# Attention scores over 64 queries of two heads and 192 keys, and a head in another order with the first group's third stage set by set

## The chip, the cores and the metric

The kernel runs on one core of one Trainium2 chip. The metric is the device time of one execution in microseconds. The profile is one further execution, taken by the hardware profiler. Of the core's engines, TensorE (PE) does the matrix products; its weight loads are listed apart as PEld. VectorE is DVE, ScalarE is ACT and GpSimd is POOL. SP only issues DMA transfers; the queues on which an engine issues them are written SPq, ACTq and so on.

## The reference

One decoder layer over 2048 tokens of width 1024, in fp32. What it computes, cut to what matters here:

```python
mod = silu(c) @ w_ada + b_ada;  shift, scale, gate = split(mod)
u = x * (1 + scale) + shift                              # (2048, 1024)
q, k, v, a_gate, p_in, p_gate, m_a, m_p = split(u @ w_in)
# 16 query heads on 2 key heads, head width 64; each query sees its last 128 keys
logits = q @ k.T / 8 + bias[query - key]; masked outside of the window
probs = softmax([logits, sink])[:-1]
a = (probs @ v * silu(a_gate)) @ w_attn_proj
p = ((pool(p_in) @ w_pool_mix) * pool_scale * silu(p_gate)) @ w_pool_proj
y = ((sigmoid(m_a) * a + sigmoid(m_p) * p) @ w_out) * (1 + gate)
out = layer_norm(alpha * x + y)
```

`silu(c) @ w_ada` is one vector times a matrix: 1024 shifts, 1024 scales and 1024 gates. The input u, and with it everything else, needs the shifts and scales first.

## The kernel before

**Products.** Every large product is done on 2 by 2 blocks with seven products in place of eight. A `Quad` holds two column tiles of 128 outputs and computes them over two halves of 512 tokens. Its moving operands are the seven `sets` B11, T1, T2, B21, T3, B22 and T4: differences and sums of the blocks of u, each held as a high and a low part (`hi`, `lo`), so that three products of reduced precision make one of full precision (`mm3`). One of the seven products is 12 instructions of 128x512. `plan` lists all products in one row of numbers; a product is the tick to which everything else is tied. The stages of a quad are F (B11, T1), S (T2, B21), Th (T3, B22) and L (T4). Quads go in groups of two or alone; in a group of two, a stage is done for the first quad and then for the second. `split_part` makes hi (ACT) and lo (DVE or POOL) of the weights some products ahead, `behind` evacuates what a product has made, and `at`, `defer` and `steps` tie other work to a product's number. Within an engine all instructions keep the order in which the program writes them.

**Phases.** The tokens go in two chunks of 1024. In each chunk there is a first phase (k, v, the first queries, two gates), an attention phase named o0 or o1 (13 quads alone, with attention laid over their products) and a phase for the rest of the projections with the pooling. After both chunks come the output projections and the layer norm.

**Attention.** `overlay` does 64 steps a chunk, one for each block of 128 queries and pair of heads. A `beat` after every quarter of a product decides when the next step comes. In `step(n)`, PE makes the scores of step n (`scores`), the transposes of step n-2 (`transposes`) and the values of step n-3 (`values`). In the program's names, `qs` are the queries, `kk` the keys (hi and lo stacked over each other on 128 partitions), `lg` the bank for scores, `bt` the bias, `L` the probabilities, `pt` the bank for transposes, `pth` and `ptl` their high and low parts, `vv` the values and `pv` the bank for the result. A step's scores are four products: two heads by hi and lo of the keys, each of 128 queries by 256 keys. ACT takes exp and scales, DVE adds the bias and finds the minimum, and makes `ptl`.

**The head.** `head` runs before the first quads and its order is written out by hand. `load(k)` fetches for each of the eight tiles of 128 channels the columns of w_ada for shift and scale and the tokens. `pe_modulation(k)` makes the tile's shifts on PE, in eight products with one moving column; in the trace they are 16 records. `modulation(k)` makes its scales on DVE, as a sum over products with `cb`, which is c spread over all partitions, and then adds the shift. Then come the modulated x, the differences, and the parts of the sets. `idle_products(n)` are n products with no use, put where PE would otherwise be idle. The products of the first two stages of the first group are written out piece by piece (`products`, `more`). After the head, `fold_parts` multiplies a pooling matrix into its weights in 16 folds, each on `pt` or `pv`, and `gate_modulation` makes the gates.

Of the kernel before, what the change touches and what calls it, by code (L numbers as in the profile page):

```python
# [19 lines left out]
P = 128  # L20
# [7 lines left out]
HD = 64  # L28
# [31 lines left out]
def kernel(  # L60
# [30 lines left out]
    BF16 = mybir.dt.bfloat16  # L91
    set_names = ("B11", "T1", "T2", "B21", "T3", "B22", "T4")
# [7 lines left out]
    nsink = cp.tile([P, HEADS], F32, name="nsink")  # L100
# [7 lines left out]
    e_rep = dp.tile([P, HEADS, ET], F32, name="e_rep")  # L108
# [24 lines left out]
    q_d = dp.tile([2, KT, 2, 2, P, CH], F32, name="q_d")  # L133
# [34 lines left out]
    class Pools:  # L168
        def __init__(self, name, **bufs):
            self.name, self.bufs, self.turns = name, {"c": 4, "p": 2, **bufs}, {}  # L170
            self.fresh = True
# [140 lines left out]
    now, due, hooks = [0], [], {}  # L312
# [139 lines left out]
    def behind(ph, q, kind, h):  # L452
        if kind == "F":
            if h == 0:
                q.c = bank(("lg", "c1")[q.x] if q.pair else "mm")
                if q.x and ph.fresh:
                    t = sets["B11"][:, 0, 0, :]
                    mm(q.c, t[:, 0:P], t, start=True, stop=True, skip_group_check=True)
                    ph.fresh = False
# [16 lines left out]
        else:  # L476
            q.consume(ph, 1, 0, q.c)

    def run(phases, products, before, loads):
        starts = {z["first"]: z for z in phases}  # L480
        ph, leave, beat = None, None, None
        for p, (q, kind, h, name) in enumerate(products):
# [29 lines left out]
            if done:  # L512
                if kind == "S":
                    behind(ph, q, kind, h)
# [3 lines left out]
            else:  # L518
# [4 lines left out]
                behind(ph, q, kind, h)  # L523
# [24 lines left out]
    def kv_quad(s):  # L548
        def keep_k(ph, t, src):
# [3 lines left out]
            defer(2, lambda: [sp.dma_start(cols(k_d[s, :, n, :], t), as32(x)) for n, x in enumerate((hi, lo))])  # L553

        def turn_v(ph, t, vt):
# [8 lines left out]
            defer(2, lambda: [sp.dma_start(v_d[s, :, a, NB * t : NB * (t + 1)], v[:, a]) for a in range(2)])  # L564

        def consume(ph, mi, t, src):
            if mi == 0:
                keep_k(ph, t, src)
            else:
                vt = ph.own("vt") if s == 0 else cols(ph.spare(), 0)  # L570
                act.activation(vt, src, AF.Copy, scale=0.5)
                defer(2, lambda: turn_v(ph, t, vt))

        return Quad((win[TK], win[TV]), consume)

    def q_quad(s, m):
        def consume(ph, mi, t, src):
            hi, lo = ph.c("q_hi", F32R), ph.c("q_lo", F32R)
            act.activation(hi, src, AF.Copy, scale=-0.125)
            dve.scalar_tensor_tensor(lo, src, -0.125, as32(hi), ALU.mult, ALU.subtract)  # L580
            defer(2 if m else 1, lambda: [sp.dma_start(q_d[s, m + mi, t, n], as32(x)) for n, x in enumerate((hi, lo))])
# [184 lines left out]
    def spread_bias(j, q):  # L766
        q.dma_start(e_rep[:, 2 * j : 2 * j + 2, :], e_d[2 * j : 2 * j + 2, :].partition_broadcast(P))

    def overlay(ph, s, n_slots):
# [4 lines left out]
        kvt, qts, bts = {}, {}, {}  # L774
        marks, Es, Ls, pts, xs, pvs, outs, ags, kept = {}, {}, {}, {}, {}, {}, {}, {}, {}
# [20 lines left out]
        def load_q(h):  # L796
# [821 lines left out]
```

## Time and profile before

| | us |
|---|---|
| median of 3 runs (lowest to highest) | 1700.26 (1699.17 to 1703.98) |
| the profiled execution | 1703.35 |
| its span in the profile | 1701.2 |
| PE busy | 1665.3 |
| first real product on PE | 22.29 |
| first and last score of the first chunk | 161.69, 471.5 |
| first and last score of the second chunk | 743.3, 1049.9 |

The profiled execution lies within the range of the three runs. In a row of the timeline there stand the start, the length from the first start to the last end, the engine, the tiles and the number of instructions. A row of grouped instructions has their busy time, the mean length of one in ns, and the idle time before them with what ended it. Almost everything goes through a helper on line 56, so tiles tell the rows apart, not lines.

### The profile page before, as it was taken

What the parts mean: (1) busy time and instruction counts of PE and PEld (TensorE: products, weight loads), DVE (VectorE), ACT (ScalarE), POOL (GpSimd) and SP (SyncE); (2) the same over time, 40 slices, a digit from 0 to 9 for tenths busy, and PEclk for the clock granted to TensorE, in tenths of its full rate; (3) what the DMA queues carried; (4) which work ended last, traced back from release to release, by engine and by line L of the source; (5) the groups of instructions that cost most, each with busy time, mean ns of one, the idle gap of its engine ahead of it and who ended that gap; (6) DMA issues with size and microseconds to landing.
All of it is one profiled execution on the core that took longest, in us unless ns stands there. A gap on an engine that the chain in (4) does not pass through costs nothing.

```text
span 1701.2 us, 24948 instructions
## 1 busy us (share of the span) xinstructions
PE 1665.3 (98%) x8112; PEld 1397.0 (82%) x8112; DVE 1185.1 (70%) x2167; ACT 988.4 (58%) x1943; POOL 589.4 (35%) x563
## 2 busy tenths in 40 slices
PE   9899999999999999999999999999999999999997
PEld 7788888888788888888888888888888888888886
DVE  6855666666647778656666666487876785778878
ACT  4645888787853336358877787333544453434553
POOL 3013454545462223323424333322242211113544
PEclk9899999999999999999999999999999999999999
DMA  9489676776557889865456454589968685777343
GB/s 358 151 294 311 202 225 217 242 239 208 170 178 223 264 288 326 289 206 157 150 171 215 156 175 135 190 280 326 329 238 309 197 312 201 261 264 281 149 149 124
DMA packets 236833, 389.50 MB, mean 229 GB/s; under 512 B 20872, under 2 KB 90528, under 8 KB 236576
## 3 DMA queue, kind: packets, MB, share of 16 engines
q1 hardware_dynamic: 231280, 382.36, 66.8%
q10 hardware_dynamic: 5392, 5.53, 1.0%
q8 instruction: 64, 1.05, 0.3%
q14 instruction: 65, 0.53, 0.1%
q0 software_dynamic: 32, 0.02, 0.0%
HBM read 243.63 MB, written 147.35 MB: 230 GB/s over the span
## 4 chain that ended last, share of the span: by engine, by line
PE 68%; ACT 11%; DVE 6%; issue 5%; DMA 3%; POOL 1%; SPq 1%; DVEq 0%; ACTq 0%; POOLq 0%
PE mm L56 43%; PE lg L56 11%; PE c L56 9%; ACT L L56 5%; PE pv L56 3%; PE pt L56 3%; DVE w_set L56 2%; ACT pth L56 2%; ACT w_set L56 1%; DVE wide L56 1%; ACT sig L56 1%; DVE p L56 1%; DVE ptl L56 1%; SPq L56 1%; ACT q_hi L56 0%
## 5 line engine op out<-in xcount | busy, mean ns | idle before, releaser
L56 PE MATMUL mm<-set_B,w_set 128*128 128x512 f32 x2664 | 652.7, 391 | 0.6 <-DVE w_set L56 0.6
L56 PEld LDWEIGHTS mm<-set_B,w_set 128*128 128x128 f32 x2664 | 496.6, 188 | 103.7 <-DVE w_set L56 1.5
L56 PE MATMUL mm<-set_T,w_set 128*128 128x512 f32 x1896 | 466.1, 392 | 1.5 <-POOL w_set L56 1.2
L56 POOL TENSOR_TENSOR W<-W 128x512 f32<-128x512 f32 x185 | 266.9, 1453 | 573.1 <-DVE w_set L56 394.0
L56 PEld LDWEIGHTS mm<-set_T,w_set 128*128 128x128 f32 x1896 | 351.5, 189 | 74.4 <-POOL w_set L56 2.5
L56 DVE TENSOR_TENSOR w_set<-W,w_set 128x1024 fp32r<-128x1024 f32 x197 | 254.5, 1292 | 110.5 <-ACT w_set L56 109.2
L56 ACT ACTIVATE L<-L 128x257 f32<-128x257 f32 (+3 forms) x512 | 241.4, 498 | 96.8 <-DVE L L56 96.3
L56 ACT CAST w_set<-W 128x1024 fp32r<-128x1024 f32 x222 | 232.2, 1047 | 97.2 <-PE mm L56 54.2
L56 PE MATMUL lg<-set_T,w_set 128*128 128x512 f32 x828 | 201.0, 391 | 2.7 <-ACT lg L56 1.7
L56 PE MATMUL c<-set_T,w_set 128*128 128x512 f32 x828 | 200.8, 391 | 0.0
L56 PEld LDWEIGHTS lg<-set_T,w_set 128*128 128x128 f32 x828 | 155.4, 188 | 36.2 <-ACT lg L56 2.1
L56 PEld LDWEIGHTS c<-set_T,w_set 128*128 128x128 f32 x828 | 155.8, 189 | 32.2
L56 DVE TENSOR_TENSOR ptl<-pt,pth 128x512 fp32r<-128x512 f32 (+1 forms) x128 | 86.4, 675 | 112.6 <-ACT pth L56 112.6
L56 POOL TENSOR_TENSOR W<-W,A 128x512 f32<-128x512 f32 x41 | 57.9, 1412 | 275.1 <-DMA A<-in_win_dram 102.7
L56 DVE CUSTOM_DVE_ANT_0 L<-lg,bt,nsink 128x256 f32<-128x256 f32 (+1 forms) x256 | 110.1, 467 | 25.1 <-PE lg L56 20.9
L56 ACT ACTIVATE sig<-mm 128x512 f32<-128x512 f32 x76 | 45.5, 599 | 94.6 <-PE mm L56 92.5
L56 PEld LDWEIGHTS lg<-kk,qs 128*128 128x128 f32 x512 | 77.4, 189 | 15.4 <-DVE L L56 4.6
L56 PE MATMUL pt<-ident,L 128*128 128x128 f32 x496 | 76.7, 276 | 9.3 <-DVE ptl L56 8.8
L56 PE MATMUL lg<-kk,qs 128*128 128x256 f32 (+1 forms) x512 | 81.5, 281 | 2.2 <-DVE L L56 1.9
L56 POOL TENSOR_TENSOR w_set<-W,w_set 128x1024 fp32r<-128x1024 f32 x25 | 61.0, 2441 | 63.7 <-ACT w_set L56 37.5
L56 PE MATMUL pv<-pth,vv 128*128 128x256 f32 x248 | 74.8, 323 | 1.1 <-DMA vv<-v_d 1.1
L56 DVE TENSOR_TENSOR st<-pv,o 64x128 f32<-64x128 f32 x256 | 71.3, 279 | 5.5 <-ACT o L56 3.8
(207 smaller groups left out, 1884.2 us busy)
## 6 DMA issues: line engine op xcount, KB each, us to landing
W<-in_win_dram SPq DMA_DIRECT2D x40, 512.0 KB, 5.8
qs<-q_d SPq DMA_DIRECT2D x128, 128.0 KB, 4.3
sums_d<-W SPq DMA_DIRECT2D x62, 256.0 KB, 4.1
W<-sums_d SPq DMA_DIRECT2D x31, 512.0 KB, 4.2
ain_d<-st SPq DMA_DIRECT2D x56, 256.0 KB, 3.5
A<-in_win_dram SPq DMA_DIRECT2D x42, 256.0 KB, 5.6
q_d<-q_hi SPq DMA_DIRECT2D x32, 256.0 KB, 4.4
q_d<-q_lo SPq DMA_DIRECT2D x32, 256.0 KB, 4.2
```

The source lines that it names most:

```text
L56: return lambda *args, **kw: self.tc.keep_in_program_order(op(*args, **kw))
```

## The change

**Scores.** A step still covers one block of 128 queries and two heads, but it is cut by queries and not by heads: each of its two halves (`eo`) holds 64 queries of both heads, stacked on 128 partitions. 64 queries see at most 192 keys, so a half's four steps (scores, minimum, exp, scaling) go over 192 columns, or 193 with the sink, in place of 256 or 257. The columns outside are zeros written once into three rooms for L. Transposes, values and all numbers of instructions stay. The queries are stored in DRAM so that 64 queries of one channel lie together (`keep_q`, `load_q`), the bias is stored for 64 partitions, the sinks are laid by head on the partitions, and `bt` has two buffers.

**Head.** c is no longer fetched again for all partitions; PE spreads it with eight products against the identity and ACT copies it. The scales of tiles 5 and 6 are made on PE like the shifts (`PE_SCALE`). The order is written anew; 32 idle products stand where 48 stood. The tail of the head casts the third stage's sets one at a time.

**First group.** The third stage goes set by set over both quads: T3, T3, B22, B22 (`woven`). Some evacuations go later (`LATER`), the folds begin four products later and end with two a product, and the stores of v in the first chunk go from ACT's queue.

```diff
+    LATER = {(0, "S"): 5, (1, "S"): 4, (1, "Th"): 5, (1, "L"): 2}
...
+                    if kind == "Th" and gi == 0 and phase.get("woven"):
+                        for x, q in enumerate(grp):
+                            q.at[kind] = p = len(products) + x
+                            stages.append((q, kind, p, p + len(grp)))
+                        products += [(q, kind, h, name) for h, name in enumerate(names) for q in grp]
+                        continue
...
-            defer(2, lambda: [sp.dma_start(v_d[s, :, a, NB * t : NB * (t + 1)], v[:, a]) for a in range(2)])
+            q = sp if s else act
+            defer(1, lambda: [q.dma_start(v_d[s, :, a, NB * t : NB * (t + 1)], v[:, a]) for a in range(2)])
...
+    def keep_q(dst, x):
+        sp.dma_start(dst.rearrange("b p c -> p b c"), x.rearrange("p (b c) -> p b c", c=HD))
...
-            q = qts[h] = tp.tile([P, 2, 2 * P], F32R, tag="qs", bufs=2, name="qs")
+            q = qts[h] = tp.tile([P, 4, 2, HD], F32R, tag="qs", bufs=2, name="qs")
             for n in range(2):
-                src = q_d[s, j, t, n][:, c * 2 * P : (c + 1) * 2 * P].rearrange("(h d) c -> d h c", h=2)
-                sp.dma_start(as32(q[n * HD : (n + 1) * HD]), src)
+                src = q_d[s, j, t, n, 4 * c : 4 * c + 4].rearrange("b (h d) c -> d (b h) c", h=2)
+                sp.dma_start(as32(q[n * HD : (n + 1) * HD]).rearrange("p b h c -> p (b h) c"), src)
...
+        def span_of(n, eo):
+            k0 = k0_of(n)
+            return (max(k0, HD), 2 * P) if eo else (k0, BAND)
...
-            for h in range(2):
+            for eo in range(2):
+                whi = q[:, n % 2 * 2 + eo].rearrange("p h c -> p (h c)")
+                k0, k1 = span_of(n, eo)
                 for hl in range(2):
                     mm(
-                        lg[:, h, k0:],
-                        q[:, h, at : at + P],
-                        kvt["k"][:, hl, (b - 1 + s) * P + k0 : (b + 1 + s) * P],
-                        start=h == 0 and hl == 0,
+                        lg[:, eo, k0:k1],
+                        whi,
+                        kvt["k"][:, hl, (b - 1 + s) * P + k0 : (b - 1 + s) * P + k1],
+                        start=eo == 0 and hl == 0,
...
-                for h in range(2):
-                    act.activation(E[:, h, e0:256], E[:, h, e0:256], AF.Copy, scale=sm[:, h : h + 1])
+                for eo in range(2):
+                    k0, k1 = span_of(n - 1, eo)
+                    x = E[:, 1 + 2 * P * eo + k0 : 1 + 2 * P * eo + k1]
+                    act.activation(x, x, AF.Copy, scale=sm[:, eo : eo + 1])
...
+    PE_SCALE = (5, 6)
...
-        sp.dma_start(cb, c.partition_broadcast(P))
...
+        for h in range(2):
+            row = bank(("pv", "pt")[h])
+            for i in range(KT // 2):
+                k = h * (KT // 2) + i
+                mm(row[:, i * P : (i + 1) * P], ct[:, k : k + 1].to_broadcast([P, P]), ident, start=i == 0, stop=True, skip_group_check=True)
+            act.copy(cols(cb, h), row)
...
-            for i in range(KT):
-                mm(sums[k][:, 0:1], ws[k][0][:, i * P : (i + 1) * P], ct[:, i : i + 1], start=i == 0, stop=i == KT - 1)
+            for n in range(2 if k in PE_SCALE else 1):
+                for i in range(KT):
+                    at_i = slice(i * P, (i + 1) * P)
+                    mm(sums[k][:, n : n + 1], ws[k][n][:, at_i], ct[:, i : i + 1], start=i == 0, stop=i == KT - 1)
```

How the change moves instructions on PE is shown at three places. In the rows, `lg`, `c`, `mm`, `pt` and `pv` are banks, `ct` is c by channel, `head_T`, `head_B` and `head_big` are the rooms for w_ada, `set_B` and `set_T` are the sets, `w_set` the split weights. The first place is PE's start up to the first real products. Before:

```order
L56 MATMUL lg<-set_B_68 128x512 x16
L56 MATMUL pv<-ct,head_T_114 128x1 x8
L56 MATMUL lg<-set_B_68 128x512 x18
L56 MATMUL pt<-ct,head_T_114 128x1 x8
L56 MATMUL lg<-set_B_68 128x512 x14
L56 MATMUL pv<-ct,head_T_115 128x1 x8
L56 MATMUL mm<-set_B_66,w_set 128x512 x3
```

Now:

```order
L56 MATMUL pv<-ident,ct 128x128 x4
L56 MATMUL pt<-ident,ct 128x128 x4
L56 MATMUL lg<-set_B_68 128x512 x8
L56 MATMUL pv<-ct,head_T_114 128x1 x8
L56 MATMUL lg<-set_B_68 128x512 x18
L56 MATMUL pt<-ct,head_T_114 128x1 x8
L56 MATMUL mm<-set_B_66,w_set 128x512 x3
```

The products with the identity stand first, the third column sum stands behind the first real product, and the fill is shorter. The second place is PE between the first and the second stage of the first group. Before:

```order
L56 MATMUL pv<-ct,head_big 128x1 x8
L56 MATMUL lg<-set_B_66 128x512
L56 MATMUL c_463<-set_B_66 128x512
L56 MATMUL lg<-set_T_159,w_set 128x512 x3
L56 MATMUL mm<-set_B_68,w_set 128x512 x3
L56 MATMUL pt<-ct,head_big_112 128x1 x8
```

Now:

```order
L56 MATMUL lg<-set_B_66 128x512
L56 MATMUL c_435<-set_B_66 128x512
L56 MATMUL pt<-ct,head_B_116 128x1 x16
L56 MATMUL pv<-ct,head_big 128x1 x16
L56 MATMUL lg<-set_T_159,w_set 128x512 x3
L56 MATMUL mm<-set_B_68,w_set 128x512 x3
```

The two doubled column sums stand together, behind the two products that open the banks. The third place is PE from the third stage of the first group to the first fold (`spare` and `room_w` are a fold's operands, `vt` is v before its transposes). Before:

```order
L56 MATMUL lg<-set_T_406,w_set 128x512 x12
L56 MATMUL mm<-set_B_565,w_set 128x512 x12
L56 MATMUL pt<-ident,vt 128x128 x4
L56 MATMUL c_463<-set_T_406,w_set 128x512 x12
L56 MATMUL pv<-spare,room_w 128x256 x12
```

Now:

```order
L56 MATMUL lg<-set_T_411,w_set 128x512 x12
L56 MATMUL c_435<-set_T_411,w_set 128x512 x12
L56 MATMUL mm<-set_B_459,w_set 128x512 x12
L56 MATMUL pt<-ident,vt 128x128 x4
L56 MATMUL mm<-set_B_459,w_set 128x512 x12
L56 MATMUL lg<-set_T_613,w_set 128x512 x12
L56 MATMUL c_435<-set_T_613,w_set 128x512 x12
L56 MATMUL pv<-ident,vt 128x128 x4
L56 MATMUL mm<-set_B_66,w_set 128x512 x12
L56 MATMUL pt<-spare,room_w 128x256 x12
```

Both T3 products come before both B22 products, the first transposes of v stand a product later, and the first fold stands behind the second group's first product.

More of the change, by code (lines that the diff above doesn't have):

```diff
@@ new lines, in head @@
+        first_cast(3)
+        modulate_x(3)
+        grp[1].mid(dve)
+        first_low(3)
+        b11_cast(3)
+        pe_modulation(4)
+        b11_low(3)
+        scale_sum(4)
+        shift_sum(4)
+        products(3, 0, 1)
+        sets["T3"] = set_tile("T3")
+        modulate_x(4)
+        cast(4, 0)
+        second_sum(4)
+        rest_of(4, 0)
+        raws = [q.second() for q in grp]
+        pairs = [cast_pair(raws[0])]
+        cast(4, 1)
+        opened[0][3] = low_pair(raws[0], pairs[0])[::-1]
@@ L1400, in head @@
+        rest_of(4, 1)
+        seed(0)
+        pairs.append(cast_pair(raws[1]))
+        t3_sum(0)
+        opened[1][3] = low_pair(raws[1], pairs[1])[::-1]
+        grp[0].late(dve)
+        seed(1)
+        pe_modulation(5)
+        shift_sum(5)
         modulate_x(5)
-        third_sums(0)()
-        products(3)
+        sets["B22"] = set_tile("B22")
         pe_modulation(6)
-        pairs = [pair_split(ph, q.second()) for q in grp]
-        for x in range(2):
-            second_pair(x, pairs[x])
+        more(0, 0)
@@ L1542, with phase @@
     phases = []
[L1544 to L1545 removed]
+    def phase(pools, groups, enter, woven=False):
+        phases.append({"pools": pools, "groups": groups, "enter": enter, "woven": woven})
     for s in range(2):
@@ L1549 @@
         if s == 0:
-            phase(Pools("g0", spare=2, x=3), start, first_start)
+            phase(Pools("g0", spare=2, x=3), start, first_start, True)
         else:
```

377 lines of the change are left out of this document (221 added, 156 removed).

## The prediction

> **What bounds the kernel now.** I read the page first: its span, its engine line and the clock line.
>
> ```profile
> span 1701.2 us, 24948 instructions
> PE 1665.3 (98%) x8112; PEld 1397.0 (82%) x8112; DVE 1185.1 (70%) x2167; ACT 988.4 (58%) x1943; POOL 589.4 (35%) x563
> PEclk9899999999999999999999999999999999999999
> ```
>
> TensorE (PE) is busy for 98% of the span. So an edit pays only where it shortens PE's own work or one of PE's few gaps. The next view is busy time by stretch: the head up to the first real product, the head's products, the rest of the first groups, and the two attention phases (columns: stretch, its length, then busy us and records of PE, PEld, DVE, ACT, POOL, then clock, DMA share, GB/s).
>
> ```profile
> 0.00:22.30 22.30, 20.61 (x97) 17.20 (x97) 11.66 (x23) 8.41 (x13) 14.05 (x40) 0.92 0.92 329
> 22.30:66.40 44.10, 42.38 (x204) 35.54 (x203) 37.39 (x62) 26.39 (x43) 0.02 (x1) 0.88 0.53 204
> 66.40:96.00 29.60, 22.13 (x123) 18.77 (x123) 22.40 (x36) 16.48 (x29) 5.86 (x4) 0.99 0.91 302
> 161.60:471.60 310.00, 301.54 (x1638) 256.81 (x1639) 198.14 (x579) 251.45 (x622) 153.96 (x174) 0.99 0.68 219
> 743.30:1050.00 306.70, 302.04 (x1672) 260.21 (x1672) 202.31 (x579) 246.35 (x608) 107.32 (x124) 1.00 0.53 172
> ```
>
> PE idles 8.5 us in the first attention phase, 4.7 us in the second and 9.2 us between 22.3 and 96 us. The table of waits says for whom.
>
> ```profile
> PE pt L56 <- DVE ptl L56: 8.8, 17, 0.7
> PE pt L56 <- ACT vt L56: 3.2, 1, 3.2
> PE pv L56 <- DVE room_small L56: 2.2, 1, 2.2
> PE lg L56 <- ACT lg L56: 1.7, 1, 1.7
> PE pv L56 <- DVE spare L56: 1.1, 1, 1.1
> PE pv L56 <- ACT spare L56: 1.0, 1, 1.0
> ```
>
> The first row is attention: transposes wait, 0.52 us at a time, until the low half of the last step's transposes has left the bank. The other five are in the head and sum to 9.2 us.
>
> **Scores on PE.** A step still has four score products; each streams 192 columns in place of 256. The trace has products of 256 and, in the first block, of 128 columns. First the groups, then one group of four of each kind in the timeline (start, length), then the weight loads.
>
> ```profile
> L56 PE MATMUL lg<-kk,qs 128*128 128x256 f32 x480 | 76.9, 283 | 1.9 <-DVE L L56 1.9
> L56 PE MATMUL lg<-kk,qs 128*128 128x128 f32 x32 | 4.6, 265 | 0.3 <-DMA qs<-q_d 0.3
> 202.52 0.63 PE L56 MATMUL lg<-kk,qs 128*128 128x256 f32 x4
> 197.43 0.56 PE L56 MATMUL lg<-kk,qs 128*128 128x128 f32 x4
> L56 PEld LDWEIGHTS lg<-kk,qs 128*128 128x128 f32 x512 | 77.4, 189 | 15.4 <-DVE L L56 4.6
> ```
>
> Busy time per product is 76.9/480 = 160 ns at 256 columns and 4.6/32 = 144 ns at 128. By starts inside a group it is (630-283)/3 = 116 ns and (560-265)/3 = 98 ns. Half the columns therefore save only 16 to 18 ns, since each product also loads 128 columns of weights (189 ns a record, partly under the product before). At 192 columns I take half of that, 8 to 10 ns, for some 500 products: **-5 us**. Bounds: 0, if the weight load alone sets the pace from 256 columns down, and 18 ns x 512 = -9 us, if 192 already costs what 128 does. Products and weight loads keep their number.
>
> **Waits in attention.** ScalarE and VectorE also handle 193 or 192 columns. Rows at both widths (of the phase, then single ones):
>
> ```profile
> L56 ACT ACTIVATE L<-L 128x257 f32<-128x257 f32 x240 | 120.5, 505 | 2.8 <-DVE L L56 2.4 <-POOL L L56 0.4
> 203.32 0.40 ACT L56 ACTIVATE L<-L 128x129 f32<-128x129 f32 x1
> L56 DVE CUSTOM_DVE_ANT_0 L<-lg,bt,nsink 128x256 f32<-128x256 f32 x240 | 105.2, 475 | 22.8 <-PE lg L56 18.6 <-POOL L L56 3.8
> 201.47 0.33 DVE L56 CUSTOM_DVE_ANT_0 L<-lg,bt,nsink 128x128 f32<-128x128 f32 x1
> ```
>
> 64 columns are half of 505-400 = 105 ns on ACT and half of 475-330 = 145 ns on DVE: about 52 and 72 ns an instruction. A step has four on ACT and two on DVE, so 0.21 and 0.14 us. This lies beside PE's work, except in the 17 waits, where two scalings stand before the cast that the transposes wait for: 0.10 us for certain, up to 0.35 us where the step's other four are also late. I take 0.2 us x 17 = **-3.4 us**; bounds -1.7 and -8.8 (all of them gone). The zero columns of L are written once, and the bias tile shrinks and gets a second buffer: no cost, since PE waits for neither tile.
>
> **The head up to the first product.** Rows: the fill, the one-column sums (16 records at full and at half clock), the first real product and the first score.
>
> ```profile
> 1.48 6.29 PE L56 MATMUL lg<-set_B 128*128 128x512 f32 x16 [1.48 <-DVE set_B L56]
> 9.75 5.97 PE L56 MATMUL lg<-set_B 128*128 128x512 f32 x18
> 15.57 1.84 PE L56 MATMUL pt<-ct,head_T 128*128 128x1 f32 x16
> 45.17 3.41 PE L56 MATMUL pt<-ct,head_big 128*128 128x1 f32 x16
> 22.29 0.96 PE L56 MATMUL mm<-set_B,w_set 128*128 128x512 f32 x3
> 161.69 0.63 PE L56 MATMUL lg<-kk,qs 128*128 128x128 f32 x4 [0.25 <-DMA qs<-q_d]
> 3.22 0.17 DVE L56 TENSOR_TENSOR ct<-ct,sg 128x8 f32<-128x8 f32 x1
> ```
>
> PE now waits for ct, ready at 3.4 us. Then, at these durations: eight identity products (fp32, so 16 records, 3.4 us on a slow start), eight fills of 0.39 us (3.1), the first sum (1.9), eighteen fills (6.0), the second sum (1.8): the first real product stands at 19.6 us against 22.3. **-2.7 us**; bounds -4 (full clock from 7 us) and +1 (the eighteen at half clock).
>
> **From there to the second group.** Added on PE: the third column sum, which stood before the first product (1.8), the doubled sums of tiles 5 and 6 (2 x 1.8) and six fills (1.4), +6.8 us. Removed: the five waits of 9.2 us. The copies that freed lg now lie behind the two doubled sums; the transposes of v come a product (2.7 us) later, and the folds four products later, as in the order below the diff. New waits: in the woven third stage both T3 products stand before both B22 products, so VectorE's last T3 casts are due 2.7 us earlier. I take +2 us; bounds 0 and +5. VectorE itself loses two column sums (and its two instructions on c); ScalarE's queue takes over the four stores of v, at the price of the store that it issues now:
>
> ```profile
> 9.77 1.28 DVE L56 CUSTOM_DVE_ANT_0 head_T<-head_T,cb,mod 128x1024 f32<-128x1024 f32 x1 [0.57 <-DMA head_T<-in_wada_dram]
> 81.03 0.41 ACTq L56 DMA_DIRECT2D wmix_d<-st  x1
> ```
>
> That is -2.4 us for VectorE and 4 x 0.41 us on ScalarE, which is busy for 16.5 of the 29.6 us there; neither sets the end. SP's queue sends the second group's weight loads ahead of the first stores of k, behind which they stood: no cost, and the cover of that group's splits grows.
>
> The clock is the last item. Before, it stayed full with one sum between products (first row), fell around 45 us, in a stretch with a wait and two column sums, and again after the wait for room_small:
>
> ```profile
> 35.00:40.00 5.00, 5.00 (x34) 4.47 (x34) 4.45 (x9) 2.13 (x5) 0.00 (x0) 1.00 1.03 411
> 45.00:50.00 5.00, 5.00 (x21) 4.61 (x21) 4.84 (x10) 3.91 (x7) 0.00 (x0) 0.50 0.41 142
> 50.00:55.00 5.00, 5.00 (x15) 3.91 (x14) 4.09 (x8) 3.25 (x7) 0.00 (x0) 0.57 0.05 17
> 95.00:100.00 5.00, 5.00 (x21) 4.50 (x22) 3.12 (x3) 1.75 (x4) 2.53 (x2) 0.66 1.01 338
> ```
>
> Half clock for about 10 + 3 us costs some 6 us there. Afterwards the 64 records of the doubled sums stand in one block: 64 x 0.115 = 7.4 us at full clock, 64 x 0.213 = 13.6 at half. I expect the clock to fall inside that block (+3.2) and to last into the products (+4), and the later fall to go with its wait: **+1 us** net, bounds -6 and +7. The Trainium skill, page "TensorE: Matmul & The Clock Gate", section "The HAM clock gate", says that an idle window of about 3.4 us halves the clock; the 0.50 above agrees. By that page the block, if it counts as idle, would halve the clock for certain, which is the first rival.
>
> Head: -2.7 + 6.8 - 9.2 + 2 + 1 = **-2 us**.
>
> **The DMA's share.** The q stores go from 128 pieces of 2 KB to 1024 of 256 bytes each, the q loads from 128 pieces of 1 KB to 512 of 256 bytes.
>
> ```profile
> q1 hardware_dynamic: 231280, 382.36, 66.8%
> q10 hardware_dynamic: 5392, 5.53, 1.0%
> qs<-q_d SPq DMA_DIRECT2D x128, 128.0 KB, 4.3
> q_d<-q_hi SPq DMA_DIRECT2D x32, 256.0 KB, 4.4
> ```
>
> Packets of 1653 bytes take 0.668 x 16 x 1701/231280 = 79 ns, those of 1026 bytes 50 ns. A 256-byte piece lies between 13 ns (in proportion) and 50 ns (as long as 1 KB). I take 16, since the two points lie nearly in proportion. In the first attention phase half the loads (64) and three of four quads' stores in a chunk (24 of 32) make 57,344 pieces: 57 us of the 16 engines against 44 before (2 KB at the same rate is 97 ns), so 0.72 of the DMA in place of 0.68: nothing. The c broadcast (512 KB) goes, which brings the first loads about 1.3 us earlier.
>
> **Sum.** -5 - 3.4 - 2 = -10.4 us. The profiled execution took 1703.35 us (2.15 around its span), 3.1 above the median 1700.26 of the runs. On its own time that is 1693; for a median, **1690 us**, of its own range 1684 to 1696.
>
> **Rivals.**
> *The clock eats the head.* The fill runs at half clock (+1 in place of -2.7) and the block takes 13.6 us with products at half clock behind it (+5 in place of +1): the head is +6, the total -2.4, about **1698 us**. For it: 0.50 where two column sums lie. Against it: the full clock with one, at 35 to 40 us.
> *The head gives all.* Doubled sums at full clock, no new wait, attention's waits gone: -7 head, -7 scores, -5 waits: **1681 us**. Against it: VectorE is busy 37.4 of 44.1 us there and has little room.
> *No gain from narrower scores.* The weight load sets the pace and PE's waits stay: only the head's -2, **1698 us**. For it: 144 ns at 128 columns.
> *Small pieces fill the DMA (the slower side).* At 50 ns the same phase would need 179 us in place of 44, a share of 1.11 in place of 0.68; PE would wait for weights and qs, and the phase would be some 34 us longer: about **1724 us**. It decides from about 40 ns a piece (share 1). Against it: the two points above; PE waits for qs once now, for 0.3 us. The Trainium skill, page "DMA: Bandwidth & Descriptors", section "Specifications", names 512 bytes as the least for line rate, with read-modify-write below; at twice my price, 32 ns (an estimate), the share would be 0.91 and the cost a few us. No run here shows such pieces yet.
>
> **How the numbers follow.** My sum 0.52; clock 0.18; all of it 0.12; no narrow gain 0.08; small pieces 0.10. What a measurement here can tell from no change is 0.3%, 5.1 us: 1695.2 to 1705.4. The first case is nearly all faster (0.49), the clock a third (0.06), the third all (0.12), the fourth hardly (0.02): faster 0.69; same 0.21; slower 0.10. The range 1680 to 1702 takes in the first four cases.
>
> **What would show it.** Groups of four scores of 0.58 to 0.61 us; 4 to 6 us in all for the waits on ptl; the first real product near 19.6 us and the first score some 2 us before its present start, 161.7; no wait for vt or room_small; PE's clock at half somewhere between 36 and 56 us; packets under 512 bytes up by 131,000 with no new wait on qs. It is wrong if the first score comes later than now, or if PE waits for DMA in the attention phases.

## The result: slower by 0.6%, and the profile after

The change takes 1712.07 us (median of 5 runs, 1710.05 to 1716.46) where the kernel before took 1701.72 (5 runs, 1699.17 to 1704.04). The ratio is 1.0064, with an interval of 1.0051 to 1.0077. The forecast was 1690 us. The profiled execution took 1711.91.

First the page of the change: span, engines, clock.

```profile
span 1710.1 us, 24991 instructions
PE 1674.4 (98%) x8146; PEld 1393.4 (81%) x8146; DVE 1163.7 (68%) x2161; ACT 963.4 (56%) x1944; POOL 592.8 (35%) x569
PEclk8899999999999999999999999999999999999999
```

PE is busy for 9.1 us longer than before, although its scores are narrower. So I cut both traces at the first and last score of each chunk (starts of products in the two timelines):

| stretch | before, us | change, us | difference |
|---|---|---|---|
| head and first group, up to the first score | 161.69 | 169.14 | +7.5 |
| first attention phase, first to last score | 309.86 | 301.65 | -8.2 |
| from there to the second chunk's first score | 271.78 | 276.16 | +4.4 |
| second attention phase | 306.52 | 301.92 | -4.6 |
| from the last score to PE's end | 642.11 | 652.03 | +9.9 |

Attention gained 12.8 us, more than the 8.4 forecast for it. The head lost 7.5; that row is the least sure one, because two traces of the same instructions have first scores some 5 us apart (below, at the clock). And 14.3 us were lost in two stretches (third and last row) where PE's products are the same as before, except for one more in each that opens a bank; besides that, only the second chunk's first stores of q differ there. Those come first. Here are 500 us of the last one in the view by stretch, before and then after:

```profile
1100.00:1600.00 500.00, 499.13 (x2201) 412.77 (x2200) 385.17 (x437) 221.01 (x287) 129.20 (x95) 1.00 0.77 265
```

```profile
1100.00:1600.00 500.00, 498.82 (x2165) 405.57 (x2164) 379.32 (x432) 219.02 (x284) 129.77 (x95) 1.00 0.76 262
```

PE is as busy in both, at full clock (1.00) in both, and gets 36 fewer products done: the products themselves are slower, by 1.7%. The grouped rows agree. Before:

```profile
L56 PE MATMUL mm<-set_B,w_set 128*128 128x512 f32 x2664 | 652.7, 391 | 0.6 <-DVE w_set L56 0.6
L56 PE MATMUL mm<-set_T,w_set 128*128 128x512 f32 x1896 | 466.1, 392 | 1.5 <-POOL w_set L56 1.2 <-DVE p L56 0.3
```

After:

```profile
L56 PE MATMUL mm<-set_B,w_set 128*128 128x512 f32 x2664 | 661.8, 394 | 1.2 <-DVE w_set L56 1.0 <-ACT w_set L56 0.2
L56 PE MATMUL mm<-set_T,w_set 128*128 128x512 f32 x1896 | 470.1, 394 | 0.6 <-POOL w_set L56 0.3 <-DVE p L56 0.2
```

The same number of products of the same shape has 9.1 and 4.0 us more of busy time. No wait accounts for it.

What do these products have in common? Sorted by where their operands lie in SBUF, they fall into two kinds. The diff has one line that seemed to be bookkeeping and that the cut diff above does not show: the tile of the sinks went from 16 columns to 8.

```diff
-    nsink = cp.tile([P, HEADS], F32, name="nsink")
+    nsink = cp.tile([P, KT], F32, name="nsink")
```

That is 32 bytes less on every partition. B11, T1 and B21 are placed ahead of it. Everything placed behind it (the other four sets, the split weights, the raw weights) stands 32 bytes lower, so the distance from a moving operand in B11, T1 or B21 to its weights has changed. For each product of 512 columns that is followed by another one (behind 100 us, gaps over 300 ns left out) I took the time from its start to the next start, by the offset: the address of the next product's weights less that of the moving operand, modulo 256 bytes.

| offset | before: products, mean ns | change: products, mean ns |
|---|---|---|
| 0 | 5420, 227.5 | 2991, 228.4 |
| 64 | - | 68, 232.2 |
| 96 | 434, 231.7 | 367, 232.2 |
| 224 | - | 2424, 233.3 |

2,424 products at 5.8 ns more and 2,991 at 0.9 more make 16.8 us. The 0.9 is carried over from the slow products: from 1100 to 1600 us the products of `set_T` into `lg`, whose own offset is 0 as before, take 235.8 ns in the first of their twelve, mostly right behind a slow one, and 226.4 to 227.0 from the eighth on. Before, all twelve took 226.6 to 226.9. This is a reading of two traces; whether the address is the cause, the experiments have to tell.

Now the head. PE's longest wait there, the first real product and the first score (rows of the timeline), and the other waits that are new:

```profile
22.09 3.54 PE L56 MATMUL pt<-ct,head_T 128*128 128x1 f32 x16 [5.94 <-DMA head_T<-in_wadat_dram]
25.50 1.63 PE L56 MATMUL mm<-set_B,w_set 128*128 128x512 f32 x3
169.14 0.63 PE L56 MATMUL lg<-kk,qs 128*128 128x64 f32 x4 [1.52 <-DMA qs<-q_d]
```

```profile
PE pv L56 <- DVE mod L56: 4.9, 1, 4.9
PE lg L56 <- DVE w_set L56: 2.0, 2, 1.7
PE lg L56 <- DMA qs<-q_d: 1.5, 1, 1.5
PE c L56 <- DVE q_lo L56: 1.4, 1, 1.4
PE pt L56 <- ACT st L56: 1.0, 1, 1.0
```

PE waits 5.94 us for the second tile's columns of w_ada, and the first real product stands at 25.50, where 19.6 were forecast. The first 30 us of the DMA view say why. In the strip each figure is the rate in one fortieth of the window, 0.75 us. Before:

```profile
GB/s 0 0 38 109 235 208 184 319 367 376 406 399 412 393 407 415 404 399 432 385 404 388 396 415 399 404 401 388 418 399 415 399 377 404 402 423 391 374 402 412
nsink<-in_sinks_dram ACTq DMA_DIRECT2D x1, 8.0 KB, 6.5
head_T<-in_relT_dram ACTq DMA_DIRECT2D x1, 2.0 KB, 6.5
```

After:

```profile
GB/s 0 0 33 175 393 306 355 126 104 126 142 93 66 71 82 55 25 39 55 58 52 160 172 257 394 377 371 355 399 371 325 377 366 377 412 393 412 432 401 421
nsink<-in_sinks_dram ACTq DMA_DIRECT2D x2, 2.0 KB, 13.4
head_T<-in_relT_dram ACTq DMA_DIRECT2D x1, 2.0 KB, 15.6
```

From 5.25 to 15.75 us the DMA moves 25 to 142 GB/s where it moved 319 to 432. In that stretch lie the two fetches of the sinks, which bring 4 KB in all. The sinks were one row of 64 bytes for each partition. Now each half of the partitions takes every second number of it, so they come in 2 x 64 x 8 = 1,024 pieces of 4 bytes:

```diff
-        act.dma_start(nsink, sinks.partition_broadcast(P))
+        by_heads = sinks.rearrange("(j h) -> h j", h=2)
...
+        for h in range(2):
+            act.dma_start(nsink[h * HD : (h + 1) * HD, :], by_heads[h].partition_broadcast(HD))
```

So there are two theories, one for each loss: **addresses** (32 bytes less slow 2,400 products) and **pieces** (1,024 tiny pieces hold up the head's loads). The rivals: that the 131,000 small packets or the new order slow TensorE, and that the head loses by its clock and its doubled sums.

### The profile page after: what moved, and what is told of

Read it like the earlier page. It is cut to its first block, busy times and chain, and to the rows that moved or that the text cites. A ratio compares the mean times of both kernels' runs of the same rounds, so it can differ in the third digit from the quotient of the medians.

```text
span 1710.1 us, 24991 instructions
## 1 busy us (share of the span) xinstructions
PE 1674.4 (98%) x8146; PEld 1393.4 (81%) x8146; DVE 1163.7 (68%) x2161; ACT 963.4 (56%) x1944; POOL 592.8 (35%) x569
## 4 chain that ended last, share of the span: by engine, by line
PE 71%; ACT 6%; DVE 4%; issue 3%; DMA 2%; POOL 0%; SPq 0%; DVEq 0%; ACTq 0%; POOLq 0%
PE mm L56 46%; PE lg L56 11%; PE c L56 9%; PE pv L56 3%; PE pt L56 2%; ACT L L56 2%; DVE wide L56 1%; DVE w_set L56 1%; ACT pth L56 1%; ACT w_set L56 1%; DVE ptl L56 1%; SPq L56 0%; ACT sig L56 0%; DMA mp_d<-sig 0%; DMA wo_d<-ux 0%
## 5 line engine op out<-in xcount | busy, mean ns | idle before, releaser
L56 PE MATMUL mm<-set_B,w_set 128*128 128x512 f32 x2664 | 661.8, 394 | 1.2 <-DVE w_set L56 1.0
L56 ACT ACTIVATE L<-L 128x193 f32<-128x193 f32 (+5 forms) x512 | 214.9, 446 | 99.2 <-DVE L L56 98.9
L56 DVE CUSTOM_DVE_ANT_0 L<-lg,bt,nsink 128x192 f32<-128x192 f32 (+2 forms) x256 | 93.9, 405 | 35.9 <-PE lg L56 26.1
L56 PE MATMUL lg<-kk,qs 128*128 128x192 f32 (+2 forms) x512 | 75.6, 270 | 3.2 <-DMA qs<-q_d 1.9
L56 ACT CAST pth<-pt 128x512 fp32r<-128x512 f32 (+1 forms) x128 | 71.8, 561 | 8.9 <-PE pv L56 7.8
```

What stands on the lines that cost most here:

```text
L56: return lambda *args, **kw: self.tc.keep_in_program_order(op(*args, **kw))
```

## Experiments on the addresses

**e1_align: the change with the old size of the tile.** One line, the sinks still in pieces:

```diff
-    nsink = cp.tile([P, KT], F32, name="nsink")
+    nsink = cp.tile([P, HEADS], F32, name="nsink")[:, 0:KT]
```

> The change as it is, with one edit: the tile of the sinks takes 16 columns again (64 bytes to a partition, of which 8 columns are used), so that every tile behind it stands at the address modulo 64 that it had in the kernel before. The sinks are still fetched in 4-byte pieces. Theory (addresses): the change made that tile 32 bytes shorter, and a 512-column product whose moving operand and weights stand in different halves of a 64-byte line takes 232 to 233 ns from start to start and not 227.5; some 3,000 products paid that. This run then takes about 1696 us (16 less than the change's 1712), its products are back at 227 ns outside attention, and from the last score to the end it takes 642 us again, not 651.6; the first score stays near 169 us. Rival (the 131,000 more small packets or the new order of attention slow TensorE): 1712, and the last stretch stays at 651.

It took 1696.26 us (ratio to before 0.9978, 0.9966 to 0.9989): 15.8 less than the change. The last stretch takes 642.98 us again, and 500 us of it hold nearly as many products as before (2201 there, 2165 in the change):

```profile
1100.00:1600.00 500.00, 498.53 (x2197) 411.86 (x2196) 383.67 (x435) 220.63 (x287) 129.37 (x94) 1.00 0.76 265
```

The first score stands at 166.96, 2 us ahead of the 169 expected. The small packets and the order are as in the change, so the rival falls.

**e4_shift: the kernel before with other addresses.** Two tiles of one column become one of 32 bytes:

```diff
-    mhalf = cp.tile([P, 1], F32, name="mhalf")
-    warm = cp.tile([P, 1], F32, name="warm")
+    small = cp.tile([P, 8], F32, name="small")
+    mhalf, warm = small[:, 0:1], small[:, 1:2]
```

> The kernel before with nothing but an address changed: two one-column tiles behind the sinks become one, so that every tile behind them stands 32 bytes lower, in the other half of 64 bytes, as in the change. No instruction, order or transfer differs. Theory (addresses): 15 to 20 us slower than before, about 1718, with 231 to 233 ns from start to start of the 512-column products whose weights and moving operand stand in different halves, and 651 us from the last score to the end. Rival (the address is of no account, and the change's slower products have another cause): 1701.7, no difference.

1714.03 us, ratio 1.0080 (1.0063 to 1.0098). The same instructions in the same order, 13.8 us slower for an address; somewhat below the 15 to 20 expected. Its last stretch takes 651.39 us, and 500 us of that stretch read as in the change:

```profile
1100.00:1600.00 500.00, 499.19 (x2167) 406.13 (x2166) 379.27 (x432) 219.12 (x284) 129.29 (x95) 1.00 0.76 262
```

**e5_all32: everything 32 bytes further.** Is a place slow, or a distance? To e3_both (below: both losses mended) a tile of 32 bytes is added ahead of all sets:

```diff
+    spacer = cp.tile([P, 8], F32, name="spacer")
```

> The kernel of e3_both with an unused tile of 32 bytes put ahead of all sets, so that every set, weight tile and raw part stands 32 bytes further: moving operands and weights of nearly all 512-column products now stand both in the upper half of 64 bytes, where in e3_both they stand both in the lower. Theory (only the offset between moving operand and weights counts): 1688 to 1693 us, within 5 of e3_both (1688.3), products at 227 to 228.5 ns from start to start. Rival (an operand in the upper half is slow by itself): 5,400 products at 4 to 5 ns more, 1709 to 1714 us.

1687.06 us, ratio 0.9920 (0.9907 to 0.9934), against 0.9927 for e3_both: no difference. 5,408 products with both operands in the upper half of 64 bytes take 227.6 ns. The distance counts, not the place.

**e9_bench and e11_bench: products alone.** No layer, only weights and a moving operand of ones.

> Not the layer at all: 16 groups of 96 products of 128x128 weights and a 512-column moving operand, both of ones, nothing else running; the output is zeros. In the groups the moving operand starts at 0, 16, 32 or 48 bytes modulo 64, and in each of these the weights at 0, 16, 32 or 48. Theory (the offset between moving operand and weights counts): about 227 ns from start to start where both start at the same offset, 232 or more where they are 32 apart, by the same amount for (0, 32) and (32, 0). Rival (an effect of what else runs in the layer): the same in all 16 groups.

The groups behind the first, in which the clock still rose, took 230.0 to 234.9 ns, and followed neither theory: (32, 32) had 231.8, (0, 32) and (32, 0) had 233.1, and (16, 32) had the least. The four slots of the weights were 576 bytes apart, so each group mixed four offsets. It decided nothing, and e11_bench puts the slots 512 bytes apart.

> Products alone again (the output is zeros), this time with the four slots of the weights 512 bytes apart as in the layer, so that the offset between moving operand and weights is one number in each group. In e9_bench the slots were 576 bytes apart, and each group mixed four offsets. 96 products to a group; the moving operand starts at 0 (14 groups), then at 32 modulo 64 (14 groups), and the weights 0, 8, 16, 32, 48, 64, 80, 96, 128, 160, 192, 224, 256 and 288 bytes further on, modulo 512. Theory (the offset alone makes the difference seen in the layer): 227 to 228 ns at 0 and 256, 231 to 234 at 32, 96, 160, 224 and 288, the same for both places of the moving operand. Rival (traffic of the layer is needed): the same in all groups.

Five groups in the timeline (97 products: 96 of the group and the last of the one before): moving operand at 0 with offsets 0, 32 and 256, then at 32 with offsets 0 and 32.

```profile
27.61 22.15 PE L56 MATMUL acc<-moving,weights 128*128 128x512 f32 x97
93.91 22.79 PE L56 MATMUL acc<-moving,weights 128*128 128x512 f32 x97
295.03 22.16 PE L56 MATMUL acc<-moving,weights 128*128 128x512 f32 x97
339.18 22.16 PE L56 MATMUL acc<-moving,weights 128*128 128x512 f32 x97
405.49 22.79 PE L56 MATMUL acc<-moving,weights 128*128 128x512 f32 x97
```

Nothing else runs here, and 0.64 us in 96 products remain: 6.7 ns for one. From start to start, the mean of each group, the same to 0.01 ns for both places of the moving operand:

| offset, bytes | 0 | 8 | 16 | 32 | 48 | 64 | 80 | 96 | 128 | 160 | 192 | 224 | 256 | 288 |
|---|---|---|---|---|---|---|---|---|---|---|---|---|---|---|
| ns | 226.7 | 230.7 | 233.3 | 233.3 | 233.3 | 233.3 | 232.0 | 234.3 | 233.4 | 233.4 | 228.9 | 233.3 | 226.7 | 233.4 |

Of the offsets tried, the fast ones are 0 and 256. At 64 and 128 the product is as slow as at 32: the period is not 64 bytes, as I had taken it; the expectation left 64 and 128 open. The 224 of the change has 233.3 ns here and there.

**e10_align_all: the 434 products that were slow before.** In every kernel so far the fifth pair of split weights in attention stood at offset 96. With three tiles of L at 528 columns for 518 it moves:

```diff
-        rooms = [tp.tile([P, 2 * 257 + 4], F32, tag=f"L{i}", bufs=1, name="L") for i in range(3)]
+        rooms = [tp.tile([P, 528], F32, tag=f"L{i}", bufs=1, name="L")[:, 0:518] for i in range(3)]
```

> e3_both with the three L tiles of attention taken at 528 columns and not 518 (the ten more stay unused): the fifth pair of split weights behind them stood at 32 modulo 64 in every kernel so far, and 428 products whose next weights lie there took 231.9 ns and not 227.5. Theory (addresses): 428 x 4.4 ns = 1.9 us less than e3_both, about 1686.4. Rival: those products are slow by what runs beside them in attention and not by the address: 1688.3, no difference.

1686.46 us, ratio 0.9923 (0.9910 to 0.9935). Against the 0.9927 of e3_both that is no difference that can be told. The trace tells more: 425 of these products now stand at offset 192 and not at 0, and take 230.3 ns where they took 231.9. That is 0.7 us. I had aligned to 64 bytes, before e11_bench said 256.

## Experiments on the sinks

**e2_sinks: the change with the sinks in rows.** Addresses as in the change:

```diff
-        by_heads = sinks.rearrange("(j h) -> h j", h=2)
...
-        for h in range(2):
-            act.dma_start(nsink[h * HD : (h + 1) * HD, :], by_heads[h].partition_broadcast(HD))
+        srow = ph.t.tile([P, HEADS], F32, tag="srow", bufs=1, name="srow")
+        act.dma_start(srow, sinks.partition_broadcast(P))
...
-        dve.tensor_scalar(nsink, nsink, -1.0, None, ALU.mult)
+        for h in range(2):
+            mine = slice(h * HD, (h + 1) * HD)
+            dve.tensor_scalar(nsink[mine, :], srow[mine, h::2], -1.0, None, ALU.mult)
```

> The change as it is, with one edit: the sinks come as one row of 64 bytes to a partition, as in the kernel before, and VectorE picks the heads of each half of the partitions at the end of the head. The addresses stay as in the change. Theory (4-byte pieces): the two fetches of the sinks, 1,024 pieces of 4 bytes, held up every load of the head behind them by 7 us; without them relT lands near 6.5 us and not 15.6, the first product of the head with its own data comes near 20 us and not 25.5, the first score near 160 us and not 169, and the run takes 1702 to 1704 us. Rival (the lower clock and the doubled sums of two tiles in one block are the head's loss, whatever the loads do): the first score stays at 167 or later, and the run at 1710 to 1712. The last stretch behind the last score stays at 651 us by both.

1702.59 us (1.0014, 1.0005 to 1.0023), 9.5 less than the change. The first score stands at 161.23, and the last stretch stays at 650.90. The rival of the clock and the doubled sums falls.

**e6_sinks_only: the kernel before with pieces.**

```diff
-        act.dma_start(nsink, sinks.partition_broadcast(P))
+        by_heads = sinks.rearrange("(j h) -> h j", h=2)
+        for h in range(2):
+            act.dma_start(nsink[0:HD, h::2], by_heads[h].partition_broadcast(HD))
+        act.dma_start(nsink[HD:, :], sinks.partition_broadcast(HD))
```

> The kernel before with one edit: the sinks of the first 64 partitions are fetched in the strided 4-byte pieces of the change (two fetches of 64 x 8 pieces into the columns of even and odd heads), those of the last 64 in rows of 64 bytes as before. Order, addresses and everything else are as before. Theory (4-byte pieces hold up the head's loads): relT lands later than 12 us (6.5 before), the first product of the head with its own data moves from 22 to 25 us or later, and the run takes 7 to 10 us more, 1707 to 1710. Rival (the pieces cost only where the head is in the new order, whose first products wait for relT): 1700 to 1702.

1708.90 us (1.0048, 1.0032 to 1.0064): 8.3 us more, with the old head. The landing times and the first real product:

```profile
nsink<-in_sinks_dram ACTq DMA_DIRECT2D x2, 2.0 KB, 13.6
nsink<-in_sinks_dram ACTq DMA_DIRECT2D x1, 4.0 KB, 15.3
head_T<-in_relT_dram ACTq DMA_DIRECT2D x1, 2.0 KB, 12.5
```

```profile
33.28 0.94 PE L56 MATMUL mm<-set_B,w_set 128*128 128x512 f32 x3
```

relT lands after 12.5 us (6.5 before), and the first real product moves from 22.29 to 33.28. The old head loses even more there than the new one, and makes part of it good later.

**e12_late: the same pieces, later.** The change with the old size of the tile, and the two fetches moved behind the sums of tile 5:

```diff
         pe_modulation(5)
         shift_sum(5)
+        for h in range(2):
+            act.dma_start(nsink[h * HD : (h + 1) * HD, :], by_heads[h].partition_broadcast(HD))
```

> The change with the tile of the sinks at 16 columns (as in e1_align), and its two fetches in 4-byte pieces left as they are but issued later, behind the sums of tile 5 (near 45 us), when the head's loads have nearly all landed. Theory (the pieces cost because the head's first loads stand beside them): 1687 to 1690 us, as e3_both without them. Rival (1,024 such pieces cost their time wherever they stand): 1694 or more.

1686.46 us (0.9921, 0.9903 to 0.9939), as fast as without pieces. They are issued at 35.25 and 36.02 us, earlier than the 45 expected, and still take 10.6 us to land:

```profile
nsink<-in_sinks_dram ACTq DMA_DIRECT2D x2, 2.0 KB, 10.6
```

Their packets start from 39.3 to 47.5 us, and SP's loads for the head end some 2 to 3 us into that; nobody waits for either. So it is the neighbourhood that costs: 1,024 pieces beside the loads that open the head. Whether their size, their number or their place on ACT's queue does it was not tried. By the Trainium skill, page "DMA: Bandwidth & Descriptors", section "Queues, rings and completion order", a DMA engine takes turns between the queues that have work for it, a whole packet at a time. That would let the pieces on ACT's queue hold up SP's loads; the runs here show that they do, and not by which rule.

## Both mended, and the change's two halves

**e3_both: the edits of e1_align and e2_sinks together.**

> Both edits in one: the tile of the sinks at 16 columns, and the sinks fetched in rows of 64 bytes. Theory (the two causes are apart from one another and add): 1686 to 1688 us, first score near 160, last stretch 642. Rival (they overlap, or only one of them counts): 1695 or more.

1688.30 us (0.9927, 0.9911 to 0.9944), 11.9 below the kernel before; the first score stands at 161.94, and the last stretch takes 642.16. The effects add: -11.9 for what the change is about, +8.0 for the pieces (e1_align less e3_both), +14.3 for the addresses (e2_sinks less e3_both), together +10.4; measured +10.35. That the two agree to a tenth is luck, because each term is uncertain by 2 to 3 us.

**e8_head: the kernel before with the new head alone.** All of the change's lines in `plan`, `run` and the head, none of attention's.

> The kernel before with the new order of the head alone (scales on TensorE with doubled sums, the first group's third stage set by set, the c row by products on TensorE), the old attention, the old sinks and the addresses as in the kernel before. Theory (removed and new waits of the head cancel, 9.7 us of waits against 7.2, and two more sums go through TensorE): 1699 to 1702 us, no difference from before. Rival (the forecast, -2 us, or the rival in which the head gives 10): 1698, or 1690.

1700.44 us (1.0005, 0.9994 to 1.0016): nothing, and the 2 us forecast lie outside of the interval. In its one trace the first score stands at 157.70, 4 us ahead of the kernel before; the runs do not show that gain.

**e7_scores: the kernel before with the new attention alone.** All of the change's lines in `overlay`, the stores of q and the bias, with the sinks in rows and the old addresses.

> The kernel before with the new attention alone: scores over 64 queries of two heads and 192 keys with all that belongs to it, the old head order, the sinks fetched in rows of 64 bytes and every address as in the kernel before. By the traces the attention of the change took 12.8 us less than before (8.2 in the first chunk, 4.6 in the second), and the head's own gain shows as nothing in e3_both (first score 161.94 against 161.69). Theory (the whole gain of 11.9 us of e3_both is the attention's): 1687 to 1690 us. Rival (the head's order gives its forecast 2 us and more): 1691 or more.

1690.42 us (0.9946, 0.9932 to 0.9959), 10.1 below before and between the two expectations (at most 1690, at least 1691). This kernel alters part of what is computed, and I did not find which part; its time is a second sign only. The first is e3_both less e8_head: about 12 us are attention's.

## Why the prediction was wrong

The forecast fell by what it did not count. **Its sum prices the edits of the program text and lets everything else keep its duration.** Two lines of the diff were given no price. The size of the tile of the sinks cost 14 to 16 us, and their fetch 8 to 9.5. The prediction's sentence on what was laid out anew in attention ("The zero columns of L are written once, and the bias tile shrinks and gets a second buffer: no cost, since PE waits for neither tile") asked who waits for a tile. It did not ask what lies behind it, nor how many pieces bring it. The sinks are not mentioned: the part on the DMA counts the pieces of q alone. With both put right, e3_both takes 1688.3 where 1690 were forecast. Some of that nearness is luck: attention's waits gave about 3 us more than forecast, and the head gave nothing in place of 2. The steps, read on e3_both:

**Scores on PE: -5, measured -6.0.** Groups and one group of four:

```profile
L56 PE MATMUL lg<-kk,qs 128*128 128x192 f32 (+2 forms) x512 | 75.5, 269 | 2.5 <-DMA qs<-q_d 1.7 <-DVE L L56 0.7
202.63 0.59 PE L56 MATMUL lg<-kk,qs 128*128 128x192 f32 x4
```

81.5 us became 75.5, and 0.63 us for four became 0.59, inside the 0.58 to 0.61 expected.

**Waits in attention: -3.4, measured -3.4 for ptl and -6.3 in all.** The waits on ptl, and the two attention phases by stretch:

```profile
PE pt L56 <- DVE ptl L56: 5.4, 13, 0.8
```

```profile
161.90:464.40 302.50, 298.22 (x1638) 256.17 (x1638) 189.43 (x578) 238.89 (x621) 153.36 (x174) 0.99 0.77 216
736.40:1037.20 300.80, 298.23 (x1669) 257.42 (x1670) 195.90 (x579) 234.41 (x608) 107.89 (x124) 1.00 0.62 171
```

ptl went from 8.8 us to 5.4: 13 waits are left of 17, at 0.42 us each in place of 0.52. But PE idled 8.5 + 4.7 us in the two phases, and now 4.3 + 2.6. The step named one wait, and some of the short ones went too. Which edit took them was not tried: the one for vv, 1.1 us, has also gone in e8_head, with the old attention. From first to last score both phases together lose 13.2 us, against 8.4.

**The head: -2, measured nothing by e8_head's runs, and +0.25 by the first score (161.94).** The runs decide, because the first score is that of one execution. In that trace two terms were off and cancel. The first real product comes at 17.61, 4.7 us earlier and not 2.7. The new waits are 7.2 us and not 2, if PE's first wait of 3.5 us for c, which only precedes the fill, is left out:

```profile
PE pv L56 <- DVE mod L56: 3.5, 1, 3.5
PE pt L56 <- ACT st L56: 1.8, 1, 1.8
PE lg L56 <- DVE w_set L56: 1.8, 2, 1.4
PE lg L56 <- DMA qs<-q_d: 1.7, 1, 1.7
PE lg L56 <- ACT w_set L56: 1.2, 1, 1.2
PE c L56 <- DVE q_lo L56: 0.7, 1, 0.7
```

-4.7 + 6.8 - 9.2 + 7.2 = +0.1. The five old waits have gone, as forecast, and other ones have come up behind them, most of them for ACT and DVE (5.5 of the 7.2 us).

**The clock: the fall came as forecast, but the one that it was set against is not always there.** It falls in the block of doubled sums:

```profile
39.66 6.61 PE L56 MATMUL pv<-ct,head_big 128*128 128x1 f32 x32
40.00:50.00 10.00, 10.00 (x40) 9.23 (x40) 5.75 (x10) 6.49 (x11) 0.00 (x0) 0.50 0.12 46
```

The second 32 records of the block take 6.61 us at half clock, though PE is busy for all of that time. In the 20 us from 40 to 60 the mean clock is 0.74, as it was in the trace of before. The later fall, which was to go with its wait, did not: from 60 to 100 us the mean clock is 0.96 in both. All eight traces with the new head have a fall that begins within the block. The old head does not have it in every trace: e4_shift has the instructions of before in the same order, and its clock stays full. Whether its addresses or chance decide that was not tried. Before, then e4_shift:

```profile
40.00:60.00 20.00, 18.31 (x72) 15.21 (x72) 16.02 (x26) 15.16 (x25) 0.00 (x0) 0.74 0.22 81
40.00:60.00 20.00, 18.91 (x92) 14.41 (x92) 18.03 (x29) 15.72 (x27) 0.00 (x0) 1.00 0.23 85
```

PE gets 92 products (column sums included) done there and not 72, and the first score of e4_shift stands at 156.78, 4.9 us ahead of the kernel before, although its addresses slow its products. So the 6 us that the forecast took for the old fall are those of one execution, and first scores that lie less than 5 us apart in single traces settle nothing.

**Small pieces of q: no cost, as forecast, at a slightly higher price.** The share of the DMA in the first phase is 0.77, where 0.72 were forecast. That is (0.77 x 302.5 - 0.68 x 310) us = 22 us of 16 engines more; with the 44 that these transfers took before, 66 x 16 / 57,344 = 18 ns a piece, where I took 16. The packets of that phase, sorted by size, say the same: 256 bytes take 18 ns at the median (20.5 in the mean), 1 KB 46 and 2 KB 84, so about 9 ns and 37 more for each KB. The Trainium skill, page "DMA: Bandwidth & Descriptors", section "Specifications", has read-modify-write below 512 bytes; the 32 ns estimated from it do not show. The rival that lets these pieces fill the DMA falls.

**What would show it wrong.** "The first score comes later than now" was named, and it came true for a reason that was in none of the cases. The other sign, waits of PE for the DMA in the attention phases, did not come in e3_both: its 1.7 us for qs stand before the first score.

## What to carry to other kernels

Before pricing a change, list which tiles move in SBUF, and by how much: where one tile shrinks, everything behind it moves, and unchanged products may change their pace. Round small tiles up, so that the distance from a moving operand to its weights stays a multiple of 256 bytes, and when unchanged phases take another time at the same clock and with no new wait, look at addresses first. Count a transfer by its pieces and by what stands beside it: 4 KB in 1,024 pieces cost 8 us at the start of the head and nothing when they were issued 33 us later.

## What the runs showed of the hardware

**The distance of the operands sets the pace of a product.** 128x128 weights and 512 columns take 226.7 ns from start to start if weights and moving operand are 0 or 256 bytes apart modulo 512, and 230 to 234 at most other distances tried (228.9 at 192), with nothing else running and for two places of the moving operand alike. The Trainium skill, page "SBUF — State Buffer", section "SBUF: two separate sides", says that PE never waits on anyone at its port, and its section "A bandwidth-pool intuition that's wrong (but worth ruling out)" gives weight loads a read port of their own. Here the two reads of one PE are not without effect on each other, or something looks the same from outside; by which part of the memory was not tried.

**Tiny pieces slow others.** With 1,024 pieces of 4 bytes in flight beside it, the DMA moved 142 GB/s from 5 to 20 us in the change, and 392 before:

```profile
5.00:20.00 15.00, 11.15 (x58) 9.71 (x58) 3.07 (x6) 3.32 (x6) 0.92 (x6) 0.94 0.44 142
```

```profile
5.00:20.00 15.00, 14.79 (x71) 12.21 (x70) 9.59 (x17) 5.39 (x9) 11.01 (x30) 0.89 1.01 392
```

That is 3.8 MB less in 15 us, or 9.6 us of transfers, near the 8 to 9.5 us that the runs lost. The share of the DMA engines' time is only 0.44 there: the engines were not full, so what held the loads up is not seen as busy time. The 1,024 packets themselves took 7.4 ns each, 7.6 us in all, which is 0.5 on each of 16 engines, but their starts are spread from 5.4 to 18.4 us.

**The clock can fall while PE is busy.** From 40 to 50 us of e3_both PE is busy for 10.00 of 10.00 us, mostly with products of one moving column, and the granted clock is 0.50. With one block of 16 such records between real products it stayed at 1.00 (35 to 40 us before); with 64 in one block it fell within the block in all eight traces with the new head.
